# Weights of a hybrid attention block: high parts by a rounding load, low parts on VectorE, and a differential score product over all 128 rows

## The chip, the cores and the metric

The kernel runs on one core of one Trainium2 chip. The metric is the time of one execution in microseconds (us) on the device; the figure of a kernel is the median of its runs. A traced execution gives a profile: a page of totals, and rows of single instructions. Line numbers L... are those of the kernel before; where the changed kernel is spoken of, they are its own (17 to 23 lower behind `weights`).

## The reference

One decoder block over 512 tokens of width 1024, in float32:

```python
xn = rmsnorm(x, norm_mix_g)
q_lat, kv_lat, k_rope, dq, dk, dv, gate_pre = split(xn @ w_in)         # 1024 -> 4256
# branch A: latent attention, 8 heads of 64 + 32 rotary, causal
q = rmsnorm(q_lat) @ mla_w_uq ;  kv = rmsnorm(kv_lat) @ mla_w_ukv
o_mla = causal_attention([q_nope, rope(q_pe)], [k_nope, rope(k_rope)], v_mla)
# branch B: differential attention, 4 heads, two maps of 64 each, V of 128
o_diff = rmsnorm(causal_attention(q1, k1, dv) - lam * causal_attention(q2, k2, dv)) * (1 - lambda_init)
gates = sigmoid(gate_pre + b_gate)
x = x + (g_mla * (o_mla @ w_branch_mla) + g_diff * (o_diff @ w_branch_diff)) @ w_out
hn = rmsnorm(x, norm_ffn_g)
x = x + (silu(hn @ w_ffn_gate) * (hn @ w_ffn_up)) @ w_ffn_down         # hidden 2816
return rmsnorm(x, norm_final_g)
```

## The kernel before

**Two-part numbers.** TensorE multiplies in a rounded 32-bit format (float32r). To keep float32 accuracy every operand is held as a pair: a high part, which is the value rounded to that format, and a low part, which is the value minus the high part. `mm3` (L298 to L302) makes three products of each pair of operands: high by high (L300), high by low (L301), low by high (L302). Activations are split by `split` (high on ScalarE at L250 or L252, low on VectorE at L254 or L256).

**Weights.** All weights but the latent projections of the start come through `weights(src, n0, n1, pick)` (L270 to L296), a tile of up to 128 x 1024 values (512 KB) at a time. SyncE (SP) loads it as it is into a float32 tile `raw`, of which there are four. `round_hi` (L261 to L265) then writes the high part into a tile `w` (`w[:, 0]`), of which there are three, on ScalarE (L263) or VectorE (L265), and `round_lo` (L268) writes the low part (`w[:, 1]`) on GpSimd or VectorE. Which engines do it is the list `w_eng`: ScalarE and GpSimd at the start, VectorE and GpSimd from the attention on, ScalarE and VectorE in the FFN. With `pick`, only some columns of the loaded tile are rounded. A block of products of one such tile is 24 times 128 x 512 (8 row blocks of the contraction, three products each). The output projection `w_out` makes its high and low parts by lines of its own (L844 to L862). The three `w` tiles hold the latent weights first (`lat_raw`), so that the first weight tiles wait for these.

**Stages.** x is loaded, normalised through its mean square only, transposed and split; the latent projections, then MLA heads in four pairs (`mla_head`), with the projections of later heads as filling work between their steps (the lists FILL and FILL_MLA: `mqk` and `pe` are the query/key parts, `mv` and `v` the values, `qk` a differential head's query and key, `gate` a gate block); then the four differential heads (`diff_head`), filled from FILL_DIFF; then branches, `w_out`, the FFN (22 pairs of gate and up blocks, the first three of which are run on the first half of the tokens ahead of the rest, `ffn_product`), the down projection in two halves of the output (`down`), and the last norm (`finish`).

**Differential heads.** `diff_qk` (L582 to L596) projects the query and key of both maps of a head (64 rows each), rotates them (`rotate`, L561 to L567, two steps of it on GpSimd), and builds per map `m`: `q[:, m]`, in which the high part of the query lies in the map's own 64 rows and, by a DMA, once more in the other 64; `k[:, m]` with the high part of the key in its own rows and the low part in the others. So one product over 128 rows gives high·high + high·low. The low part of the query lies in `ql[own]` alone, and a second product over 64 rows gives low·high. `scores` (L627 to L645, the product at L636) runs both for each of four row blocks of 128, 256, 384 and 512 keys, for both maps; VectorE masks and takes the maximum (L640), ScalarE the exponential (L155), VectorE the reciprocal (L643) and joins the two maps (L688, L689).

**What sets the order.** The kernel's text is put into one instruction stream per engine by a scheduler that simulates a timeline; `urgent()` gives attention steps precedence. Each engine and each DMA queue works through its stream in order. A tile's name is used again in turn (L 22 buffers, raw 4, w 3, P 6, t 5; in PSUM mm 3, sc 2, tr 2, pv 1): a writer waits until the last reader of the buffer's previous content is done.

Of the kernel before, what the change touches and what calls it, by code (L numbers as in the profile page):

```python
# [13 lines left out]
F32R = mybir.dt.float32r  # L14
# [7 lines left out]
P = 128  # L22
# [22 lines left out]
W_DVE = "b0 b1 b2 b3 b4 b5 b6 b7".split()  # L45
N_WARM = 8
P_POOL = (0, 1)
W_ENG0 = ['act', 'pool']
W_ENG = ['dve', 'pool']
# [43 lines left out]
def build(ctx, nc, tc, a, out):  # L93
# [9 lines left out]
    def T(tag, shape, dtype):  # L103
        return sb.tile(shape, dtype, name=nm(tag), tag=tag, bufs=BUFS[tag])
# [16 lines left out]
    def r32(ap):  # L121
        return ap.bitcast(F32)

    def dma(o, i):
        nc.sync.dma_start(out=o, in_=i)
# [130 lines left out]
            nc.vector.scalar_tensor_tensor(out=lo, in0=src, scalar=scale, in1=r32(hi),  # L256
                                           op0=ALU.mult, op1=ALU.subtract)

    w_eng = list(W_ENG0)

    def round_hi(o, i):  # L261
        if w_eng[0] == 'act':
            nc.scalar.activation(out=o, in_=i, func=AF.Copy)  # L263
        else:
            nc.vector.tensor_copy(out=o, in_=i)  # L265

    def round_lo(o, i, hi):
        (nc.vector if w_eng[1] == 'dve' else nc.gpsimd).tensor_sub(out=o, in0=i, in1=r32(hi))  # L268

    def weights(src, n0, n1, pick=None):  # L270


        raw = T("raw", [P, 1024], F32)
        n = n0 * n1
        rv = raw[:, :n].rearrange("p (a b) -> p a b", a=n0)
        if isinstance(src, list):
            for i, s_ in enumerate(src):
                dma(rv[:, i, :].rearrange("p (h d) -> p h d", h=s_.shape[1]), s_)
        else:
            dma(rv, src)  # L280
        w = T("w", [P, 2, 1024], F32R)
        if pick is None:
            round_hi(w[:, 0, :n], raw[:, :n])
            round_lo(w[:, 1, :n], raw[:, :n], w[:, 0, :n])
        else:
            nk = sum(h * (d1 - d0) for h, d0, d1 in pick)
            wv = [w[:, s, :n0 * nk].rearrange("p (a b) -> p a b", a=n0) for s in range(2)]
            c = 0
            for h, d0, d1 in pick:
                src_ = rv.rearrange("p a (h e) -> p a h e", h=h)[:, :, :, d0:d1]  # L290
                hi, lo = [v[:, :, c:c + h * (d1 - d0)].rearrange("p a (h e) -> p a h e", h=h) for v in wv]
                c += h * (d1 - d0)
                round_hi(hi, src_)
                round_lo(lo, src_, hi)
            n = n0 * nk
# [286 lines left out]
    def diff_qk(h):  # L582


        u = diff_project(C_DQ + h * P)
        q, k = L_(), L_()
        if h % 2 == 0:
            q_lo.append(L_())
        ql = q_lo[-1][:, h % 2, :]
        for m, own, other in ((0, low, high), (1, high, low)):  # L590
            split(u[own], q[own, m, :], ql[own], DIFF_SCALE)
            dma(r32(q[other, m, :]), r32(q[own, m, :]))
        u = diff_project(C_DK + h * P)
# [4 lines left out]
    q_lo = []  # L598


    dv = []
# [207 lines left out]
    for p in range(4):  # L809
        o = L_()  # L810
        o_mla.append(o)
        w_eng[:] = W_ENG
        fill(FILL_MLA[p])
        with urgent():
            for h in range(2):
                mla_head(mqk[p], mv[p // 2], p, o, h)
# [62 lines left out]
                norm_transpose(x1[t], g_ffn, hn, t, T("L", [P, D], F32))  # L879


    w_eng[:] = ["act", "dve"]
# [119 lines left out]
```

## Time and profile before

| | |
|---|---|
| median of 3 runs | 767.74 us (767.48 to 768.22) |
| the profiled execution, its own time | 767.65 us |
| its span, from first to last instruction | 765.3 us |
| TensorE clock granted | 0.998 |
| instructions | 9589 |
| bytes read from HBM | 69.81 MB |

A row of the page's first part gives an engine's busy time, its share of the span and its instructions; PE is TensorE, PEld its weight loads, DVE VectorE, ACT ScalarE, POOL GpSimd, SP SyncE. The rows of groups give line, engine, operation, tiles written and read with their shapes, how many, then busy time and the mean of one in ns, then idle time ahead of them with what ended it. The table of windows gives the same busy times for stretches of the span, and a timeline row the start and duration of single instructions; matmuls overlap in it by their pipeline, so that the distance from start to start is what one costs.

### The profile page before, as it was taken

How to read it: one execution, taken by the hardware profiler on the slowest of the kernel's cores; microseconds unless marked ns; L12 is line 12 of the kernel's file. 1: busy time of each engine (PE TensorE's matmuls, PEld its weight loads, DVE VectorE, ACT ScalarE, POOL GpSimd, SP SyncE). 2: the span in 40 equal slices, each digit the busy share in tenths (PEclk: the TensorE clock that was granted, in tenths of full speed). 3: DMA queues.
4: the chain of work that ended last, by engine and by line, in shares of the span. 5: the costliest groups of instructions: out<-in, count | busy, mean ns of one | idle time of the engine just before them, and what ended most of it. 6: DMA issues, size and time to landing. Idle time of an engine off the chain costs nothing.

```text
span 765.3 us, 9589 instructions
## 1 busy us (share of the span) xinstructions
PE 747.1 (98%) x3639; PEld 620.6 (81%) x3639; DVE 429.9 (56%) x800; ACT 293.7 (38%) x567; POOL 167.0 (22%) x120
## 2 busy tenths in 40 slices
PE   8999999999999999999999999999999999999996
PEld 6888899887676788888889888888888888888884
DVE  6969698888999874568363333233323332223424
ACT  7464667553443421724243323232222323122314
POOL 3405343664563454430000000000000000000302
PEclk9999999999999999999999999999999999999999
DMA  9405342523222322327422332323232323232302
GB/s 309 108 1 142 98 120 72 136 69 80 72 70 57 82 83 82 110 85 253 103 83 72 94 110 83 110 83 111 83 110 83 110 85 108 87 105 87 107 0 110
DMA packets 99179, 75.67 MB, mean 99 GB/s; under 512 B 6175, under 2 KB 86845, under 8 KB 99133
## 3 DMA queue, kind: packets, MB, share of 16 engines
q1 hardware_dynamic: 99133, 75.07, 33.3%
q8 instruction: 28, 0.46, 0.3%
q14 instruction: 18, 0.15, 0.1%
HBM read 69.81 MB, written 2.10 MB: 94 GB/s over the span
## 4 chain that ended last, share of the span: by engine, by line
PE 81%; DVE 12%; issue 3%; DMA 1%; ACT 1%; POOL 1%; SPq 1%; DVEq 0%; POOLq 0%; ACTq 0%
PE ps_mm L301 22%; PE ps_mm L300 22%; PE ps_mm L302 22%; PE ps_sc L636 2%; DVE L L256 1%; PE ps_sc L301 1%; PE ps_tr L301 1%; PE ps_sc L302 1%; PE ps_tr L300 1%; PE ps_tr L302 1%; PE ps_sc L300 1%; DVE L L254 1%; PE ps_tr L662 1%; DVE w L265 1%; DVE P L688 1%
## 5 line engine op out<-in xcount | busy, mean ns | idle before, releaser
L301 PE MATMUL ps_mm<-X,w 128*128 128x512 f32 (+1 forms) x568 | 217.9, 384 | 0.0
L300 PE MATMUL ps_mm<-X,w 128*128 128x512 f32 (+1 forms) x568 | 217.7, 384 | 0.0
L302 PE MATMUL ps_mm<-X,w 128*128 128x512 f32 (+1 forms) x568 | 217.3, 383 | 0.0
L268 DVE TENSOR_TENSOR w<-raw,w 128x1024 fp32r<-128x1024 f32 x66 | 82.3, 1248 | 161.1 <-ACT w L263 161.0
L263 ACT ACTIVATE w<-raw 128x1024 fp32r<-128x1024 f32 (+1 forms) x72 | 74.0, 1031 | 160.0 <-issue 78.9
L268 POOL TENSOR_TENSOR w<-raw,w 128x1024 fp32r<-128x1024 f32 (+3 forms) x48 | 102.5, 2139 | 118.5 <-DVE w L265 36.1
L301 PEld LDWEIGHTS ps_mm<-X,w 128*128 128x128 f32 x568 | 106.9, 188 | 21.1 <-issue 0.7
L300 PEld LDWEIGHTS ps_mm<-X,w 128*128 128x128 f32 x568 | 106.7, 188 | 21.2 <-issue 1.2
L302 PEld LDWEIGHTS ps_mm<-X,w 128*128 128x128 f32 x568 | 106.9, 188 | 20.5 <-issue 0.4
L937 POOL TENSOR_TENSOR L<-L,P 128x512 f32<-128x512 f32 (+1 forms) x9 | 11.5, 1297 | 410.2 <-ACT t L936 410.1
L155 ACT ACTIVATE P<-P,sm 128x128 f32<-128x128 f32 (+3 forms) x64 | 35.9, 562 | 60.3 <-DVE sm L640 60.1
L911 DVE TENSOR_TENSOR t<-t,ps_mm 128x512 f32<-128x512 f32 x22 | 15.1, 688 | 59.7 <-PE ps_mm L302 59.7
L636 PE MATMUL ps_sc<-L,L 96*128 96x128 f32 (+11 forms) x160 | 42.6, 347 | 3.8 <-DVE sm L640 3.8
L910 ACT ACTIVATE t<-ps_mm 128x512 f32<-128x512 f32 x22 | 13.2, 599 | 80.8 <-PE ps_mm L302 80.8
L636 PEld LDWEIGHTS ps_sc<-L,L 96*128 96x128 f32 (+2 forms) x160 | 26.7, 188 | 14.8 <-issue 6.2
L301 PE MATMUL ps_mm<-w,L 128*128 128x512 f32 (+1 forms) x100 | 37.2, 372 | 0.0
L300 PE MATMUL ps_mm<-w,L 128*128 128x512 f32 (+1 forms) x100 | 37.2, 374 | 0.0
L302 PE MATMUL ps_mm<-w,L 128*128 128x512 f32 (+1 forms) x100 | 37.1, 373 | 0.0
L265 DVE CAST w<-raw 128x1024 fp32r<-128x1024 f32 (+3 forms) x42 | 36.0, 856 | 1.8 <-PE ps_mm L302 1.4
L250 ACT ACTIVATE L<-t 64x512 fp32r<-64x512 f32 (+2 forms) x47 | 29.2, 625 | 17.0 <-POOL t L566 7.3
L301 PE MATMUL ps_mm<-L,w 128*128 128x512 f32 x90 | 35.5, 394 | 0.0
L254 DVE TENSOR_TENSOR L<-t,L 128x512 fp32r<-128x512 f32 (+2 forms) x37 | 33.2, 897 | 4.0 <-ACT L L250 3.6
(264 smaller groups left out, 1269.2 us busy)
## 6 DMA issues: line engine op xcount, KB each, us to landing
raw<-w_in SPq DMA_DIRECT2D x28, 512.0 KB, 3.9
raw<-w_ffn_gate SPq DMA_DIRECT2D x22, 512.0 KB, 3.9
raw<-w_ffn_up SPq DMA_DIRECT2D x22, 512.0 KB, 3.9
raw<-w_ffn_down SPq DMA_DIRECT2D x22, 512.0 KB, 3.6
raw<-w_out SPq DMA_DIRECT2D x8, 512.0 KB, 3.6
L<-L SPq DMA_DIRECT2D x24, 128.0 KB, 2.3
L<-x SPq DMA_DIRECT2D x8, 256.0 KB, 5.7
raw<-w_branch_mla SPq DMA_DIRECT2D x4, 512.0 KB, 3.4
```

The costliest lines, as they stand in the source:

```text
L155: return nc.scalar.activation(**kw)
L250: nc.scalar.activation(out=hi, in_=src, func=AF.Copy, scale=scale)
L254: nc.vector.tensor_sub(out=lo, in0=src, in1=r32(hi))
L263: nc.scalar.activation(out=o, in_=i, func=AF.Copy)
L265: nc.vector.tensor_copy(out=o, in_=i)
L268: (nc.vector if w_eng[1] == 'dve' else nc.gpsimd).tensor_sub(out=o, in0=i, in1=r32(hi))
L300: nc.tensor.matmul(out=o, lhsT=lh, rhs=rh, start=start, stop=False)
L301: nc.tensor.matmul(out=o, lhsT=lh, rhs=rl, start=False, stop=False)
L302: return nc.tensor.matmul(out=o, lhsT=ll, rhs=rh, start=False, stop=stop)
L636: nc.tensor.matmul(out=ps[:, :n], lhsT=q[:, i * P:n], rhs=k[:, 0:n], start=j == 0, stop=j == last)
L910: last_silu = nc.scalar.activation(out=g, in_=gate_ps, func=AF.Silu)
L911: nc.vector.tensor_mul(out=g, in0=g, in1=ps)
```

## The change

`weights` loads every tile twice: the high part comes by a DMA on GpSimd's queue that writes float32 into the float32r tile `w[:, 0]` and rounds on the way; the float32 values come by SyncE into `raw` as before; VectorE makes every low part (L278). `round_hi`, `round_lo`, `w_eng`, W_ENG0 and W_ENG are gone. With `pick` only the needed columns are loaded, one DMA per row block of the contraction and queue. The rest of the loads keep their engines. `diff_qk` builds the low part of the query like the high part: in the map's own 64 rows and, by a DMA, in the other 64, in a tile of its own per head (before, two heads shared one); the second product runs over 128 rows, against the same `k[:, m]`, and so adds low·low as well.

```diff
-    w_eng = list(W_ENG0)
-
-    def round_hi(o, i):
-        if w_eng[0] == 'act':
-            nc.scalar.activation(out=o, in_=i, func=AF.Copy)
-        else:
-            nc.vector.tensor_copy(out=o, in_=i)
-
-    def round_lo(o, i, hi):
-        (nc.vector if w_eng[1] == 'dve' else nc.gpsimd).tensor_sub(out=o, in0=i, in1=r32(hi))
-
     def weights(src, n0, n1, pick=None):
...
         raw = T("raw", [P, 1024], F32)
+        w = T("w", [P, 2, 1024], F32R)
+        if pick is not None:
+            (heads, d0, d1), = pick
+            n1 = heads * (d1 - d0)
         n = n0 * n1
...
-            dma(rv, src)
-        w = T("w", [P, 2, 1024], F32R)
-        if pick is None:
-            round_hi(w[:, 0, :n], raw[:, :n])
-            round_lo(w[:, 1, :n], raw[:, :n], w[:, 0, :n])
...
+        for t, eng in ((w[:, 0, :n], nc.gpsimd), (raw[:, :n], nc.sync)):
+            v = t.rearrange("p (a b) -> p a b", a=n0)
+            if pick is not None:
+                for i in range(n0):
+                    eng.dma_start(out=v[:, i, :].rearrange("p (h d) -> p h d", h=heads),
+                                  in_=src[:, i, :].rearrange("p (h e) -> p h e", h=heads)[:, :, d0:d1])
+            elif isinstance(src, list):
+                for i, s_ in enumerate(src):
+                    eng.dma_start(out=v[:, i, :].rearrange("p (h d) -> p h d", h=s_.shape[1]), in_=s_)
+            else:
+                eng.dma_start(out=v, in_=src)
+        nc.vector.tensor_sub(out=w[:, 1, :n], in0=raw[:, :n], in1=r32(w[:, 0, :n]))
...
         u = diff_project(C_DQ + h * P)
-        q, k = L_(), L_()
-        if h % 2 == 0:
-            q_lo.append(L_())
-        ql = q_lo[-1][:, h % 2, :]
+        qs, k = [L_(), L_()], L_()
         for m, own, other in ((0, low, high), (1, high, low)):
-            split(u[own], q[own, m, :], ql[own], DIFF_SCALE)
-            dma(r32(q[other, m, :]), r32(q[own, m, :]))
+            split(u[own], qs[0][own, m, :], qs[1][own, m, :], DIFF_SCALE)
+            for q in qs:
+                dma(r32(q[other, m, :]), r32(q[own, m, :]))
...
-        return [[(q[:, m, :], k[:, m, :]), (ql[own], k[own, m, :])] for m, own in ((0, low), (1, high))]
+        return [[(q[:, m, :], k[:, m, :]) for q in qs] for m in range(2)]
```

GpSimd's stream at the end of the start, before: `w_772` is the rotary query tile (`pe`, group 0), `w_800` the second gate block, `w_831` the first values of MLA, the two 128x384 and 128x256 rows the query and key tiles of head pairs.

```order
L268 TENSOR_TENSOR w_740<-raw_738,w_740 128x256
L268 TENSOR_TENSOR w_772<-raw_768,w_772 128x384
L268 TENSOR_TENSOR w_800<-raw_798,w_800 128x1024
L268 TENSOR_TENSOR w_831<-raw_829,w_831 128x512
L268 TENSOR_TENSOR w_873<-raw_871,w_873 128x384
L268 TENSOR_TENSOR w_892<-raw_890,w_892 128x256
L268 TENSOR_TENSOR w_912<-raw_910,w_912 128x1024
```

The same place in the changed kernel, where `w_775` is the rotary query tile, `w_807` the second gate block, `w_838` the first values of MLA and `w_927` the first of the two tiles of differential values (`v`, number 0):

```order
L271 DMA w_743<-mla_w_ukv 128x2x64 x2
L275 DMA w_775<-mla_w_uq 128x4x32 x3
L277 DMA w_807<-w_in 128x8x128
L271 DMA w_838<-mla_w_ukv 128x4x64 x2
L271 DMA w_882<-mla_w_uq 128x2x64 x3
L271 DMA w_905<-mla_w_ukv 128x2x64 x2
L277 DMA w_927<-w_in 128x4x256
```

Where GpSimd subtracted, it now starts the loads of the high parts, tile by tile in the same succession; each of them waits for its buffer of `w`.

TensorE's stream where the rotary query tile is first used, before (`w_721` and `w_740` are the query and key tiles of the first head pair, `w_772` the rotary one):

```order
L302 MATMUL ps_mm_724<-L_640,w_721 128x512
L300 MATMUL ps_mm_743<-L_700,w_740 128x512
L300 MATMUL ps_mm_775<-L_624,w_772 128x512
L301 MATMUL ps_mm_775<-L_624,w_772 128x512
L302 MATMUL ps_mm_775<-L_624,w_772 128x512
L300 MATMUL ps_mm_775<-L_632,w_772 128x512
L301 MATMUL ps_mm_775<-L_632,w_772 128x512
```

And in the changed kernel (`w_720`, `w_743`, `w_775`):

```order
L285 MATMUL ps_mm_728<-L_640,w_720 128x512
L283 MATMUL ps_mm_749<-L_700,w_743 128x512
L283 MATMUL ps_mm_783<-L_624,w_775 128x512
L284 MATMUL ps_mm_783<-L_624,w_775 128x512
L284 MATMUL ps_mm_749<-L_700,w_743 128x512
L285 MATMUL ps_mm_749<-L_700,w_743 128x512
```

The rotary tile's first products stand at the same place, behind the query products of the first head pair and one key product; what moved is that the rest of the key products now stands among its own.

TensorE's stream in the changed kernel at the FFN's fourth product (`w_4093` is the tile of the third, `w_4201` that of the fourth; the third is the last that runs in two halves of 256 tokens):

```order
L285 MATMUL ps_mm_4097<-X_3707,w_4093 128x256
L283 MATMUL ps_mm_4097<-X_3707,w_4093 128x256
L284 MATMUL ps_mm_4097<-X_3707,w_4093 128x256
L285 MATMUL ps_mm_4097<-X_3707,w_4093 128x256
L283 MATMUL ps_mm_4205<-X_3706,w_4201 128x512
L284 MATMUL ps_mm_4205<-X_3706,w_4201 128x512
```

The succession is that of before; the buffer that `w_4201` takes is that of the first of the three tiles, whose last product stands 35 rows of 256 columns ahead of the first one here.

More of the change, by code (lines that the diff above doesn't have):

```diff
@@ L47 @@
 P_POOL = (0, 1)
-W_ENG0 = ['act', 'pool']
-W_ENG = ['dve', 'pool']
 FILL = [[("gate", 0, 0)], [], [("pe", 0), ("mr", 0), ("gate", 0, 1), ("mv", 0)]]
@@ L274, in weights @@
+        if pick is not None:
+            (heads, d0, d1), = pick
+            n1 = heads * (d1 - d0)
         n = n0 * n1
[L275 to L279, printed above, removed]
-            dma(rv, src)
-        w = T("w", [P, 2, 1024], F32R)
-        if pick is None:
-            round_hi(w[:, 0, :n], raw[:, :n])
-            round_lo(w[:, 1, :n], raw[:, :n], w[:, 0, :n])
[L285 to L295, printed above, removed]
+        for t, eng in ((w[:, 0, :n], nc.gpsimd), (raw[:, :n], nc.sync)):
[9 more added lines that the diff above has]
+                eng.dma_start(out=v, in_=src)
@@ L595, in diff_qk @@
             split(u[own], k[own, m, :], k[other, m, :])
-        return [[(q[:, m, :], k[:, m, :]), (ql[own], k[own, m, :])] for m, own in ((0, low), (1, high))]
-    q_lo = []
+        return [[(q[:, m, :], k[:, m, :]) for q in qs] for m in range(2)]
     dv = []
@@ L811, in build @@
         o_mla.append(o)
-        w_eng[:] = W_ENG
         fill(FILL_MLA[p])
@@ L879, in build @@
                 norm_transpose(x1[t], g_ffn, hn, t, T("L", [P, D], F32))
-    w_eng[:] = ["act", "dve"]
     def ffn_product(ps, w, c0, c1):
```

## Prediction

> **What bounds the kernel now.** I read the page's totals first, then a table of stages, then what each engine does in the stage where TensorE has company. From the page: the busy totals, the clock, the DMA queues and the chain that ended last.
>
> ```profile
> PE 747.1 (98%) x3639; PEld 620.6 (81%) x3639; DVE 429.9 (56%) x800; ACT 293.7 (38%) x567; POOL 167.0 (22%) x120
> ...
> PEclk9999999999999999999999999999999999999999
> ...
> q1 hardware_dynamic: 99133, 75.07, 33.3%
> ...
> PE 81%; DVE 12%; issue 3%; DMA 1%; ACT 1%; POOL 1%; SPq 1%; DVEq 0%; POOLq 0%; ACTq 0%
> ```
>
> TensorE is busy 747.1 of 765.3 us at an undiminished clock, so time is won by shortening its products or by filling its last 18 us, and lost wherever it is made to wait. The windows by stage (window, its length, then busy us of PE, PEld, DVE, ACT, POOL, clock, DMA share, GB/s) say where it isn't alone: start, MLA, differential attention, gates and branches, FFN.
>
> ```profile
> 0.00:50.00 50.00, 44.60 (x257) 37.69 (x258) 38.29 (x119) 32.55 (x88) 16.42 (x26) 1.00 0.51 160
> ...
> 75.00:150.00 75.00, 73.22 (x488) 67.01 (x487) 61.36 (x152) 48.76 (x116) 31.75 (x29) 1.00 0.43 111
> 150.00:280.00 130.00, 126.36 (x566) 96.08 (x565) 117.50 (x238) 53.93 (x128) 68.55 (x37) 1.00 0.28 72
> 280.00:420.00 140.00, 139.97 (x708) 119.27 (x708) 77.98 (x120) 51.31 (x87) 28.99 (x13) 1.00 0.35 110
> 420.00:640.00 220.00, 220.00 (x973) 182.15 (x972) 75.50 (x81) 64.57 (x81) 0.00 (x0) 1.00 0.33 98
> ```
>
> From 150 to 280 us VectorE has 117.5 of 130 us and TensorE idles 3.6; from 75 to 150 TensorE idles 1.8. In the FFN it idles not at all. In that crowded stage the groups of GpSimd and VectorE are:
>
> ```profile
> L268 POOL TENSOR_TENSOR w<-raw,w 128x1024 fp32r<-128x1024 f32 x16 | 40.4, 2524 | 37.8 <-DVE sm L643 15.8 <-DVE w L265 9.8 <-issue 7.2
> L265 DVE CAST w<-raw 128x1024 fp32r<-128x1024 f32 x16 | 13.7, 858 | 0.3 <-PE ps_mm L302 0.3
> L688 DVE TENSOR_SCALAR P<-P,sm,neg_lam 128x384 f32<-128x384 f32 x4 | 8.1, 2016 | 0.1
> L688 DVE TENSOR_SCALAR P<-P,sm,neg_lam 128x512 f32<-128x512 f32 x4 | 2.9, 736 | 0.0
> L256 DVE SCALAR_TENSOR_TENSOR L<-t,L 64x512 fp32r<-64x512 f32 x6 | 10.3, 1708 | 0.2 <-ACT L L250 0.2
> L256 DVE SCALAR_TENSOR_TENSOR L<-t,cols,L 128x512 fp32r<-128x512 f32 x2 | 1.5, 748 | 0.0
> ```
>
> The same L688 takes 2.02 us on 384 columns and 0.74 on 512, and L256 1.71 us on 64 partitions against 0.75 on 128: VectorE operations are stretched where GpSimd's 2.5-us subtractions lie beside them.
>
> **Second score product, 128 rows instead of 64.** The timeline of TensorE (start, us, operation) shows a 128-row product and its 64-row companion as one row "x2", on 512, 384, 256 and 128 columns, each with what follows:
>
> ```profile
> 266.71 0.82 PE L636 MATMUL ps_sc<-L,L 128*128 128x512 f32 x2
> 267.46 0.50 PE L300 MATMUL ps_mm<-X,w 128*128 128x512 f32 x1
> 267.79 0.39 PE L301 MATMUL ps_mm<-X,w 128*128 128x512 f32 x1
> 268.02 0.39 PE L302 MATMUL ps_mm<-X,w 128*128 128x512 f32 x1
> ...
> 260.42 0.70 PE L636 MATMUL ps_sc<-L,L 128*128 128x384 f32 x2
> 261.06 0.50 PE L301 MATMUL ps_mm<-X,w 128*128 128x512 f32 x1
> ...
> 226.78 0.59 PE L636 MATMUL ps_sc<-L,L 128*128 128x256 f32 x2
> 227.30 0.50 PE L301 MATMUL ps_mm<-X,w 128*128 128x512 f32 x1
> ...
> 253.60 0.47 PE L636 MATMUL ps_sc<-L,L 128*128 128x128 f32 x2
> 254.00 0.50 PE L707 MATMUL ps_tr<-L,ones_r 128*128 128x512 f32 x1
> ```
>
> From start to start an ordinary 512-column product takes 268.02 − 267.79 = 0.23, two of them 0.46; the pair takes 267.46 − 266.71 = 0.75, so 0.29 too much. For 384, 256 and 128 columns the pair takes 0.64, 0.52 and 0.40; by columns two ordinary ones would take 0.35, 0.23 and 0.12; that is 0.29, 0.29, 0.29 and 0.28 too much, and I take 0.18 for the last, since so short a product may not shrink in full proportion. Four heads with two maps make eight pairs of each size: 8 × 1.05 = 8.4 us. The product behind a pair comes 0.10 late too (267.46 to 267.79 is 0.33 for 0.23), at most 32 × 0.10 = 3.2 more; which of the two kinds of product costs it the trace doesn't say, so I take half. Sum −10.0 (bounds −8.4 and −11.6). The additional q copies (eight more of 128 KB on SP) have many microseconds until their scores; I cost them at nothing, 1 us if a head came tight.
>
> The Trainium skill, page "TensorE: Matmul & The Clock Gate", section "Packing small matmuls — row/col tiling", states that products in different row groups overlap, starting about 4 ns apart. That speaks against this edit. One place in the trace has both 64-row products side by side:
>
> ```profile
> 172.58 0.70 PE L636 MATMUL ps_sc<-L,L 128*128 128x256 f32 x3
> 173.21 0.50 PE L301 MATMUL ps_mm<-X,w 128*128 128x512 f32 x1
> ```
>
> Three products in 0.63 us, where a pair alone took 0.52: there the second half-height one was nearly free. If it held everywhere, three products would do the work of four in 16 blocks, and the edit would cost 16 × about 0.16 (the mean of 0.11 to 0.23) = 2.5 us; the four pairs above contradict it, since the order parts the two halves, and I give that 0.02.
>
> **Low parts from GpSimd to VectorE.** GpSimd loses 40.4 us between 150 and 280; VectorE loses 13.7 us of casts and gains 16 subtractions. Their duration, and the high parts that ScalarE made, from the page's groups:
>
> ```profile
> L268 DVE TENSOR_TENSOR w<-raw,w 128x1024 fp32r<-128x1024 f32 x66 | 82.3, 1248 | 161.1 <-ACT w L263 161.0
> L263 ACT ACTIVATE w<-raw 128x1024 fp32r<-128x1024 f32 (+1 forms) x72 | 74.0, 1031 | 160.0 <-issue 78.9
> ```
>
> 16 × 1.25 = 20.0. Stretching that goes is at least 4 × 1.28 (L688) + 6 × 0.96 (L256) = 10.9. So VectorE goes from 117.5 to at most 113, in a stage that TensorE wants to run through in 120: it keeps pace, barely. Of the 5.4 us that TensorE idles from 75 to 280 I take back 2 (bounds 0 and 5.4), since the chain runs through VectorE there. ScalarE loses 74 us that lay beside products: nothing.
>
> **High parts by a rounding load.** Before, the float32 tile lay in SBUF ahead of time in one of four raw buffers; once a w buffer (three) came free only 1.03 us (L263) or 0.86 (L265) and the subtraction stood ahead of the products. Now the load itself waits for the w buffer. A block needs L + 1.25 − 0.23 between that release and its first product (L from trigger to landing; one high·high product runs ahead of the low part), about 0.75 less for the small MLA tiles. Nothing of before loads on GpSimd's queue or converts on the way; the nearest rows (KB each, us to landing) are
>
> ```profile
> raw<-w_ffn_gate SPq DMA_DIRECT2D x22, 512.0 KB, 3.9
> ...
> L<-x SPq DMA_DIRECT2D x4, 512.0 KB, 8.0
> ...
> raw<-mla_w_uq SPq DMA_DIRECT2D x6, 64.0 KB, 3.8
> ```
>
> 3.9 is the same tile without conversion and alone, 8.0 a tile of that size in the crowded start, which also includes waiting behind others. I take L = 5.0, nearer the first, since the queues have room (33.3%), and keep 3.9 and 8.0. The Trainium skill, page "DMA: Bandwidth & Descriptors", fits loads issued by GpSimd with 2.0 us + bytes / 436e3, an estimate of 3.2 us here; by that only pe0 below would wait, 0.4 us, and the sum would come to about 756.
>
> Most leads are long: an FFN block is 24 products, 24 × 0.23 = 5.5 us, and the buffer of the block before last is released two blocks ahead, 10.9; the differential tiles have 11 to 15. With L = 5.0 a wide tile needs 6.0, and these don't wait. The short leads, counted from the changed order's products by these durations:
>
> - pe0's tile takes the buffer of the first gate block. In the trace of before:
>
> ```profile
> 54.54 0.39 PE L302 MATMUL ps_mm<-X,w 128*128 128x512 f32 x1
> ...
> 58.19 0.62 PE L300 MATMUL ps_mm<-L,w 128*128 128x512 f32 x2
> ```
>
>   release at 54.77 (54.54 + 0.23), first use 58.2: 3.4 us, 3.1 in the new order; need 5.3: +2.2.
> - v0's first tile: lead 4.5, need 6.0: +1.5.
> - MLA tiles: two wide ones with 5.5 and 5.7: +0.8.
> - FFN's fourth product: its buffer comes free 35 half-width products ahead, 35 × 0.12 = 4.2; need 6.0: +1.8. Two rows of that spacing, in the FFN's first blocks:
>
> ```profile
> 408.83 0.28 PE L300 MATMUL ps_mm<-X,w 128*128 128x256 f32 x1
> 408.95 0.28 PE L301 MATMUL ps_mm<-X,w 128*128 128x256 f32 x1
> ```
>
> - Three blocks where the down projection changes halves: lead 5.5, need 5.35 (four high products ahead): nothing, with no margin.
> - The first gate block's load starts beside x and the latents:
>
> ```profile
> 0.00:19.00 19.00, 15.77 (x84) 11.43 (x84) 13.03 (x43) 14.16 (x38) 7.18 (x17) 1.00 0.91 309
> ```
>
>   with the DMA engines at 91%: +0.7 (0 to 1.7).
>
> VectorE gets a new wait: each low part stands in its queue for the landing, and softmax steps, rotations and evictions queue behind it, for which score products wait. Sixteen times a fraction of a microsecond against 7 us of slack: +1.0 (0 to 6). GpSimd's queue, where the load stands where L268 stood, waits for the same release and is freed sooner than by 2.5 us of work: nothing.
>
> Sum: −10.0 − 2.0 + 2.2 + 1.5 + 0.8 + 1.8 + 0.7 + 1.0 = −4.0. The profiled execution took 767.65 (span 765.3 and 2.35 around it), 0.09 under the median of 767.74: **763.7**.
>
> **Rivals.** Each microsecond of L adds one at five places, and beyond 5.5 also at the other MLA tiles and the three blocks of the down projection.
>
> - *Faster still, about 758.* L = 3.9: the waits shrink to about 2.5, all else as above. For it: the queues are two thirds empty. Chance 0.15.
> - *The load comes late (slower).* L = 6.5: pe0 3.7, v0 3.0, k1 1.3, the other MLA tiles 4, fourth product 3.3, the down blocks 3 × 1.2, start 0.7, VectorE 2, about 21 against −12: **777**. L = 8 adds 1.5 at about twelve tiles: 795. It decides from L of about 5.5. For it: the 8.0 row, a conversion on the way, a second stream of the same size beside it; against it: 3.9. The Trainium skill, page "SBUF — State Buffer", names it the "DVE blocks DMA" trap: a DMA issued from GpSimd cannot get its descriptors written while VectorE holds their shared port in a 2-port mode. What it would do here lies within L; no run of before has such loads. Chance 0.34, with the overlap case above 0.36.
> - *No change.* VectorE at 113 of 120, waiting for landings, sets the pace of the differential stage, so that 4 to 5 of the 10 us there stay idle: 767 to 769. Chance 0.14.
> - *Throughput.* The weights are read twice now, so 33.3% becomes about 67% if both kinds of packet cost the same. If rounding packets took three times a plain one's time, 33% + 99% would be over capacity and the FFN would stretch by a third, beyond 880. Chance 0.05.
>
> The forecast has 0.30.
>
> **How the numbers follow.** A measurement here can tell 0.2% (1.5 us). Faster 0.30 + 0.15 = 0.45; same 0.14; slower 0.36 + 0.05 = 0.41. The range leaves out what is below 757, the far end of the late load above 785 and the throughput case, together about 0.2: 757 to 785. As both signs hold much, the likeliest case alone goes from 760 (L 4.4) to 766 (L 5.3).
>
> **What would show it.** Right: differential score pairs 0.46 apart on 512 columns; L688 at 0.7 us everywhere; TensorE idle before pe0, v0 and FFN's fourth product, and nowhere else in the FFN; rounding loads near 5 us. Wrong: landings above 5.5 us, idle time before many tiles put down to low parts (L278), or VectorE waiting on landings from 150 to 280.

## The result, and the profile after

The changed kernel takes 775.1 us (median of 5 runs, 772.5 to 777.51), the kernel before in the same comparison 768.22 (767.48 to 769.64): a ratio of 1.0089, 95% interval 1.0069 to 1.0109. It is slower by 6.9 us, where 763.7 was forecast; the time is inside the stated range, and the sign is that of the rival "the load comes late" (777).

The profiled execution took 775.42 us, with a span of 773.6. From its page, the lines that answer to those of before: busy totals, the clock, the two DMA queues.

```profile
PE 741.9 (96%) x3639; PEld 622.2 (80%) x3639; DVE 417.9 (54%) x806; ACT 224.3 (29%) x495; POOL 169.9 (22%) x204
...
PEclk9999999999999999999999999999999999999998
...
q0 software_dynamic: 93760, 55.71, 39.1%
q1 hardware_dynamic: 104093, 74.68, 35.2%
```

TensorE is busy 5.2 us less (747.1 before) but stands idle 31.7 of 773.6 us, where it stood 18.2. The stages, in the same windows as before (the differential stage and what follows lie some microseconds later now):

```profile
0.00:50.00 50.00, 43.42 (x248) 36.76 (x249) 39.97 (x118) 28.34 (x79) 16.89 (x29) 1.00 0.62 165
50.00:75.00 25.00, 23.19 (x124) 18.76 (x124) 19.62 (x40) 9.14 (x20) 8.20 (x11) 1.00 0.71 111
75.00:150.00 75.00, 68.66 (x451) 62.13 (x450) 53.73 (x138) 45.51 (x107) 21.90 (x34) 0.98 0.92 157
150.00:280.00 130.00, 125.64 (x614) 104.22 (x613) 108.09 (x255) 58.16 (x138) 46.19 (x42) 0.99 0.78 155
...
420.00:640.00 220.00, 220.00 (x972) 182.14 (x971) 75.43 (x80) 25.26 (x40) 34.64 (x40) 1.00 0.91 195
```

In the FFN nothing waits, as forecast, although the DMA engines are shown 91% busy. In the MLA stage (75 to 150) TensorE idles 6.3 us instead of 1.8. VectorE's busy time between 150 and 280 fell from 117.5 to 108.1, but its queue now stands at low parts for loads. What VectorE waited for from 160 to 300 us (us in total, times, longest):

```profile
DVE w L278 <- DMA w<-w_in: 19.3, 10, 4.7
```

The same of TensorE in the whole span:

```profile
PE ps_mm L283 <- DMA w<-w_in: 3.6, 3, 2.2
PE ps_sc L615 <- DMA L<-L: 3.2, 2, 2.0
PE ps_sc L615 <- DVE sm L619: 2.2, 2, 2.0
...
PE ps_mm L283 <- DMA w<-w_ffn_up: 1.3, 1, 1.3
PE ps_mm L285 <- DVE w L278: 1.3, 2, 0.8
...
PE ps_sc L283 <- DMA w<-w_ffn_down: 1.1, 1, 1.1
```

The first, fourth and sixth are waits for the new loads themselves, the fifth for low parts that stand behind such a load; with two smaller rows of that kind (0.5 and 0.2) they sum to 8.0 us. The second is for copies between rows of SBUF that stay on SyncE's queue, the third for softmax on VectorE. The landings (KB each, median us from issue):

```profile
raw<-w_in SPq DMA_DIRECT2D x28, 512.0 KB, 4.3
w<-w_in POOLq DMA_DIRECT2D x28, 512.0 KB, 5.8
...
w<-w_ffn_down POOLq DMA_DIRECT2D x22, 512.0 KB, 4.1
L<-L SPq DMA_DIRECT2D x32, 128.0 KB, 4.4
...
w<-mla_w_uq POOLq DMA_DIRECT2D x18, 64.0 KB, 2.4
```

Wide rounding loads of w_in take 5.8 us where 5.0 was assumed; the small ones are faster than assumed, 2.4, though their two or three issues stand one behind the other. The copies between SBUF rows went from 2.3 to 4.4.

All kernels issue 3639 products in nearly the same succession, so the start of the n-th product shows where time goes. Worked out from the traces, in us from the span's start; "joint" is the kernel of the experiments below with plain loads, all low parts on VectorE and 128 rows (e3_low_on_vector):

```
n        before  changed  joint   what is near it
50         14.0     14.4   14.4   start
300        57.6     59.5   57.2   first MLA projections
400        75.9     83.2   76.4   first MLA head
850       144.2    155.5  144.2   last MLA head
1400      271.2    272.2  257.0   last differential head
2100      411.8    413.7  401.2   ahead of FFN's fourth product
2200      431.6    435.8  421.1   behind it
3300      681.0    685.1  670.4   ahead of the down projection's change of halves
3500      726.3    732.4  715.7   behind it
last      757.6    763.7  747.0
```

Against before, the changed kernel loses 11.3 us up to the last MLA head, wins 10.3 back in the differential stage, and loses 0.9 in the stages behind it, 2.3 at the FFN's fourth product, 2.0 at the change of halves and 2.2 behind the last product (9.9 us to the end, 7.7 before). In that end the last two additions stand in VectorE's order behind the third token block's last steps: they start at 765.76, 1.7 us after the last product, where they started with it before.

### The profile page after: what moved, and what is told of

Same layout as the page of the kernel before. It is cut to its first block, busy times and chain, and to the rows that moved or that the text cites. A ratio compares the mean times of both kernels' runs of the same rounds, so it can differ in the third digit from the quotient of the medians.

```text
span 773.6 us, 9788 instructions
## 1 busy us (share of the span) xinstructions
PE 741.9 (96%) x3639; PEld 622.2 (80%) x3639; DVE 417.9 (54%) x806; ACT 224.3 (29%) x495; POOL 169.9 (22%) x204
## 4 chain that ended last, share of the span: by engine, by line
PE 42%; issue 9%; DMA 3%; DVE 2%; ACT 0%; DVEq 0%; POOLq 0%; ACTq 0%
PE ps_mm L285 11%; PE ps_mm L283 11%; PE ps_mm L284 11%; DMA w<-w_ffn_down 1%; PE ps_sc L284 1%; PE ps_sc L285 1%; PE ps_sc L283 1%; PE ps_tr L284 1%; PE ps_tr L283 1%; PE ps_tr L285 1%; DVE w L278 1%; DMA w<-w_ffn_up 1%; DMA w<-w_ffn_gate 1%; PE ps_pv L284 0%; PE ps_pv L283 0%
## 5 line engine op out<-in xcount | busy, mean ns | idle before, releaser
L278 DVE TENSOR_TENSOR w<-raw,w 128x1024 fp32r<-128x1024 f32 (+2 forms) x114 | 131.7, 1155 | 251.8 <-DMA w<-w_ffn_up 76.0
L277 POOL DMA_DIRECT2D w<-w_ffn_gate x22 | 19.3, 876 | 139.9 <-PE ps_mm L285 139.8
L277 POOL DMA_DIRECT2D w<-w_ffn_up x22 | 19.2, 873 | 111.4 <-PE ps_mm L285 111.4
L615 PE MATMUL ps_sc<-L,L 96*128 96x128 f32 (+7 forms) x160 | 37.7, 335 | 5.5 <-DMA L<-L 3.2
L277 POOL DMA_DIRECT2D w<-w_in x28 | 25.2, 901 | 69.2 <-PE ps_mm L285 45.9
L252 DVE TENSOR_TENSOR L<-t,L 128x512 fp32r<-128x512 f32 (+2 forms) x37 | 28.9, 783 | 14.7 <-ACT L L248 14.3
L277 POOL DMA_DIRECT2D w<-w_ffn_down x22 | 15.7, 711 | 94.0 <-PE ps_sc L285 36.3
L284 PE MATMUL ps_mm<-L,w 128*128 128x512 f32 x90 | 35.3, 394 | 0.0
L285 PE MATMUL ps_mm<-L,w 128*128 128x512 f32 x90 | 35.2, 393 | 0.0
L283 PE MATMUL ps_mm<-L,w 128*128 128x512 f32 x90 | 35.1, 391 | 0.0
```

Source lines behind the costliest of these rows:

```text
L252: nc.vector.tensor_sub(out=lo, in0=src, in1=r32(hi))
L277: eng.dma_start(out=v, in_=src)
L278: nc.vector.tensor_sub(out=w[:, 1, :n], in0=raw[:, :n], in1=r32(w[:, 0, :n]))
L283: nc.tensor.matmul(out=o, lhsT=lh, rhs=rh, start=start, stop=False)
L284: nc.tensor.matmul(out=o, lhsT=lh, rhs=rl, start=False, stop=False)
L285: return nc.tensor.matmul(out=o, lhsT=ll, rhs=rh, start=False, stop=stop)
```

## The experiments

The first theory after the result (A) was that the score product gives its 10 us and that the loads cost more than was worked out. Its rival (B) was that the time won came from GpSimd's subtractions going. A third (C) was that two streams of loads slow each other.

**Which part gains.** The kernel before with the new `diff_qk` alone (e1_rows128):

```diff
-        return [[(q[:, m, :], k[:, m, :]), (ql[own], k[own, m, :])] for m, own in ((0, low), (1, high))]
+        return [[(q[:, m, :], k[:, m, :]) for q in qs] for m in range(2)]
```

> The kernel before with the second score product over 128 rows alone; loads, high and low parts as before. Theory A (the score product gives what was worked out, the loads cost more than worked out): 757 to 760, differential score pairs on 512 columns 0.46 us apart, nothing else moved. Theory B (the time won between 155 and 272 us came from GpSimd's subtractions going, not from the score product): 765 to 768.

Measured: 765.43 us, ratio 0.9972 (0.9961 to 0.9983), 2.2 us better than before's 767.64 in that comparison. Theory A falls in the form it was put. The changed kernel with `diff_qk` of before (e2_loads_rows64):

> The changed kernel with the second score product back on 64 rows; rounding loads and low parts on VectorE stay. Theory A: 775 plus 8 to 11, so 783 to 786. Theory B: 774 to 777.

Measured: 778.85, ratio 1.0143 (1.0125 to 1.0162); against the changed kernel's 775.1 the 128 rows are worth 3.8. Next, e1 with every low part on VectorE (e3_low_on_vector):

```diff
-W_ENG0 = ['act', 'pool']
-W_ENG = ['dve', 'pool']
+W_ENG0 = ['act', 'dve']
+W_ENG = ['dve', 'dve']
```

> Rows 128 as in the first run, plain loads and high parts as before, but every low part on VectorE as in the changed kernel. Theory A: VectorE's relief from GpSimd is worth 0 to 3 us beyond the first run, 755 to 760. Theory B: it carries the gain, 5 to 10 us below the first run. If VectorE becomes the bound: 2 to 8 above the first run.

Measured: 756.14, ratio 0.9843 (0.983 to 0.9857), 9.3 below e1. And the same line in the kernel before, with 64 rows (e8_low_on_vector_rows64):

> The kernel before with every low part on VectorE and nothing else. Theory B with VectorE as the pace of the differential stage: with GpSimd out of the way TensorE is the limit there, so the score product over 64 rows costs its 8 to 10 us, 764 to 766 against 756.1 with 128 rows. If the score product is worth the 2 to 4 us of the two other comparisons everywhere: 758 to 760.

Measured: 763.47, ratio 0.9946 (0.9931 to 0.996). So the rows alone give 2.2, the low parts alone 4.7 (768.13 in that comparison), both together 11.5. With GpSimd out of the way the score product is worth 7.3, otherwise 2.2. The stage shows why: from 150 to 280 us in e1,

```profile
150.00:280.00 130.00, 120.44 (x575) 97.83 (x575) 117.96 (x239) 54.70 (x130) 68.61 (x37) 0.99 0.33 82
```

TensorE's work shrank (126.36 before), VectorE's didn't, and TensorE waits for it. Its waits from 150 to 300 us in e1:

```profile
PE ps_sc L632 <- DVE sm L636: 7.1, 6, 1.5
PE ps_tr L658 <- DVE P L685: 2.0, 1, 2.0
```

And in e3, where those are all of them:

```profile
PE ps_tr L703 <- DVE L L695: 2.5, 1, 2.5
PE ps_mm L300 <- DVE t L564: 1.2, 1, 1.2
```

The six waits for softmax are gone in e3, although VectorE does 22.2 us of subtractions more. The groups of VectorE from 150 to 280 us show what paid for it, first in e1:

```profile
L256 DVE SCALAR_TENSOR_TENSOR L<-t,L 64x512 fp32r<-64x512 f32 x6 | 10.3, 1710 | 0.2 <-ACT L L250 0.2
L684 DVE TENSOR_SCALAR P<-P,sm,neg_lam 128x384 f32<-128x384 f32 x4 | 8.1, 2022 | 0.1
```

Then the same lines and the subtractions in e3:

```profile
L268 DVE TENSOR_TENSOR w<-raw,w 128x1024 fp32r<-128x1024 f32 x17 | 22.2, 1303 | 0.1
L256 DVE SCALAR_TENSOR_TENSOR L<-t,L 64x512 fp32r<-64x512 f32 x6 | 5.9, 986 | 0.1
L684 DVE TENSOR_SCALAR P<-P,sm,neg_lam 128x384 f32<-128x384 f32 x4 | 1.9, 478 | 0.1
```

L684 falls from 2.02 to 0.48 us, L256 from 1.71 to 0.99. Summed over all operations in 150 to 280, what VectorE needs beyond the shortest of each kind is about 31 us in e1 and about 10 in e3. That agrees with the Trainium skill, page "SBUF — State Buffer", section "Who interferes with whom", by which a VectorE operation with two SBUF inputs, or in a two-port mode, and a GpSimd operation that reads SBUF exclude each other.

**Where the loads lose.** The rest, 775.1 − 756.14 = 19.0 us, is what the rounding loads cost. Three kernels use them in one part of the program only, plain loads elsewhere:

```diff
+    cast = [True]
+    def weights(*args):
+        return (weights_cast if cast[0] else weights_raw)(*args)
...
+    cast[0] = False
     o_diff, parts = [], []
```

That is e10_cast_to_mla, on the basis of e3:

> 128 rows, low parts on VectorE, rounding loads for the tiles up to the last MLA head alone (the first two differential heads' tiles among them), plain loads behind. From the traces' common places (the same count of products) the changed kernel has lost 11 of its 19 us by 144 us: 766 to 769 against 756.1 if that loss arises there. If it is made up for later, because VectorE has slack: 758 to 763.

Measured: 766.58, ratio 0.9983 (0.997 to 0.9996): 10.4 above e3. The differential heads, gates and branches alone, with `cast` true from that last line to the FFN (e11_cast_diff_branches):

> The same, rounding loads for the tiles of the last differential heads, gates and branches alone. If VectorE's waits for landings (19.3 us in ten waits between 160 and 300 us of the changed kernel) set the pace there: 759 to 763, with idle TensorE put down to VectorE between 160 and 280. If leads of 11 to 15 us hide them, as was forecast: 755 to 757.

Measured: 760.78, ratio 0.9905 (0.9892 to 0.9917): 4.6 above e3. From 150 to 300 us its TensorE waits for rotations on VectorE, which itself stands 17.8 us for loads of w_in between 160 and 300:

```profile
PE ps_mm L329 <- DVE t L593: 5.7, 3, 3.0
```

From the FFN on, with `cast` true from there, on the basis of e1 (e4_cast_from_ffn):

> Rows 128, the weights of before up to the branches, rounding loads from the FFN on. Theory A: first run plus 2.1 (FFN's fourth product) plus 2 (change of halves in the down projection) plus at most 2.2 (end), 761 to 765. If the second stream of loads cost throughput by itself: more, with idle time spread over the FFN's blocks.

Measured: 770.87, ratio 1.004 (1.0028 to 1.0053): 5.4 above e1's 765.43. The three add up to 20.4, close to the 19.0; of e4's 5.4, 1.0 stands at its start already, where its traced run waits longer for x (2.42 us for 1.68 in e1).

The products' starts and the spans say the same of the changed kernel itself. Against e3 it loses 11.3 us up to the 850th product and a net 1.2 from there to the 2100th: 3.9 are lost by the 1400th, and 2.7 come back behind it, where e3 has a wait of its own (2.5 us, for the rounded squares of the last differential head). It loses 2.2 more at the FFN's fourth product, 2.0 at the change of halves and 2.7 behind the last product: 19.4 in all (773.6 − 754.2).

**What they lose by.** e6_four_high divides the w tile and gives the high part a fourth buffer for one raw tile:

```diff
-BUFS = dict(X=2, L=22, P=6, PT=1, raw=4, w=3, t=5, sm=24)
+BUFS = dict(X=2, L=22, P=6, PT=1, raw=3, wh=4, wl=3, t=5, sm=24)
...
-        w = T("w", [P, 2, 1024], F32R)
+        wh, wl = T("wh", [P, 1024], F32R), T("wl", [P, 1024], F32R)
```

> The changed kernel with the w tile divided in a high tile (four of them) and a low tile (three), and three raw tiles instead of four, so that each rounding load may start one block earlier in the same memory. Theory A (the loads lose by waiting for a buffer): the waits ahead of the rotary tile, the differential values, the first differential query, FFN's fourth product and the down projection's change of halves go or shrink, 775 becomes 760 to 766. Theory C (two streams of loads slow everything): 772 or more, waits on plain copies stay.

Measured: 767.75 (763.45 to 771.22), ratio 0.9996 (0.9978 to 1.0013): 7.3 us of the 19 come back. In its trace no wait stands at the FFN's fourth product or at the change of halves, and from 160 to 300 us VectorE waits for no rounding load (19.3 us in the changed kernel); from the 850th to the 1400th product it loses nothing against e3, where the changed kernel loses 3.9. So from the differential stage on the loads lose by waiting for their buffer. Most of the time that comes back is behind that stage: 2.3 at the fourth product, 2.0 at the change of halves and 2.7 behind the last product. Of the 3.9, 3.2 are lost again by the 2100th product, most of it in a wait of 2.33 at the output projection, where VectorE stands for a late load of x. Up to the 850th product e6 loses 11.6, as much as the changed kernel. That doesn't clear the buffers there, since the low part still has three: at 62.06 us VectorE has stood 2.17 us for one, and TensorE then waits 2.29 us for the rotation behind it, in the place where the changed kernel waits for a load.

e7_small_as_before loads the small MLA tiles as before:

```diff
+        small = pick is not None or isinstance(src, list)
+        return (weights_raw if small else weights_cast)(src, n0, n1, pick)
```

> The changed kernel with the small MLA tiles (picked columns, rotary tile) loaded whole and rounded as before, low parts on VectorE; wide tiles keep their rounding loads. If the three or two serial issues of GpSimd per small tile and their short runs carry the loss between 58 and 145 us: 766 to 770. If the wide tiles carry it: 773 to 776.

Measured: 773.4, ratio 1.0071 (1.0053 to 1.0088): 1.7 below the changed kernel, with intervals that overlap. At the 300th product it has lost 0.9 us against e3, the changed kernel 2.3; by the 850th 10.0. The small tiles are at most a small part of it.

e12_copies_on_act_queue moves the copies between SBUF rows to ScalarE's DMA queue:

```diff
+    def copy_rows(o, i):
+        nc.scalar.dma_start(out=o, in_=i)
...
-                dma(r32(q[other, m, :]), r32(q[own, m, :]))
+                copy_rows(r32(q[other, m, :]), r32(q[own, m, :]))
...
-            dma(r32(q[64:96, :, :]), r32(pe[r0:r0 + 32, :, :]))
-            dma(r32(k[64:96, :, :]), r32(kpe))
+            copy_rows(r32(q[64:96, :, :]), r32(pe[r0:r0 + 32, :, :]))
+            copy_rows(r32(k[64:96, :, :]), r32(kpe))
```

> The changed kernel with the copies between SBUF rows (rotary rows of MLA, both halves of the differential query) on ScalarE's DMA queue instead of SyncE's. If the copies are late because they queue behind raw loads that wait for a raw tile, whose release waits for a low part and that for a rounding load: both waits of TensorE for them (1.95 and 1.27 us) go, 769 to 772. If they are late because the DMA engines are crowded: 774 to 777, the waits stay.

Measured: 775.1 (771.9 to 778.79), ratio 1.0086 (1.0059 to 1.0113). The two waits for copies are gone from its trace, so the queue was their cause (the copies land no sooner, 4.7 us for 4.4, but start earlier); at the 900th product it is 3.9 us ahead of the changed kernel; the median time is the same. A wait of 1.50 us for w_in at 86 us (the second tile of the first differential values), one of 1.77 for softmax at 183 and one of 1.82 for VectorE at 275 stand in their place. So this expectation was right on the cause and missed the time. The median decides little here: three of the six runs took 771.9 to 773.1 us at a granted clock of 0.992 to 0.995, three 777.1 to 778.8 at 0.985 to 0.987. The traced one is among the longer, with five slow stretches as described below (near 68, 184, 276, 420 and 706 us), where the changed kernel's has two.

e9_second_stream was to measure a second stream by itself, into one spare tile that nobody reads, in turn rounding and plain:

```diff
+            spare = spare if streams[0] % 2 else r32(spare)
+            nc.gpsimd.dma_start(out=spare.rearrange("p (a b) -> p a b", a=n0), in_=src)
```

> The kernel with plain loads, 128 rows and low parts on VectorE (756.1), and beside it a second load of every wide tile on GpSimd's queue into a spare tile that nobody reads, in turn rounding and plain; L tiles 21 instead of 22. It measures the second stream by itself. Theory A: nothing waits for it, 755 to 759; landings of the plain loads on SyncE's queue 4 to 5 us instead of 3.9. Theory C: 762 or more, with TensorE waiting for plain copies. A rounding load lands later than a plain one on the same queue by 0 to 1 us.

Measured: 849.8, ratio 1.1063 (1.1035 to 1.1091). This experiment was badly made: with one spare tile each load waits for the one before, and GpSimd's other work queues behind:

```profile
PE ps_tr L663 <- POOL P L775: 21.2, 4, 14.4
PE ps_tr L663 <- ACT P L777: 9.8, 2, 5.3
PE ps_tr L708 <- POOL L L701: 8.1, 3, 4.5
```

It says nothing on the two streams, but one thing on the rounding: in the down projection rounding and plain loads alternate on GpSimd's queue, and eleven in a row landed after 5.0, 5.5, 5.4, 5.0, 4.9, 5.0, 4.9, 6.1, 5.4, 5.2 and 5.0 us. All 22 lie between 4.7 and 6.1; the two kinds average 5.2 and 5.1. Rounding costs nothing that shows. GpSimd's queue is slower than SyncE's in this run (3.6 there), but not in general: in the changed kernel w_ffn_up lands after 4.7 us on GpSimd's queue and 5.4 on SyncE's, w_ffn_down after 4.1 and 4.2.

Four more kernels went at the 10.4 us up to the last MLA head, on the basis of e10. One more w tile, with 20 L tiles instead of 22 to make room (e14_four_w), and its control with plain loads (e14_plain_l20):

```diff
-BUFS = dict(X=2, L=22, P=6, PT=1, raw=4, w=3, t=5, sm=24)
+BUFS = dict(X=2, L=20, P=6, PT=1, raw=4, w=4, t=5, sm=24)
```

> Rounding loads up to the last MLA head (766.6) with four w tiles instead of three, raw still four, L 20 instead of 22 to make room. If the loads lose by waiting for a w tile: 757 to 761, if the plain kernel with 20 L tiles stays near 756. If by crowding or VectorE's queue: 764 to 767.

> The plain kernel with low parts on VectorE and 128 rows (756.1) with 20 L tiles: the control of the run before. 755 to 758 if the two tiles aren't missed.

Measured: 771.78, ratio 1.0062 (1.0045 to 1.0079), and 766.62, ratio 0.9986 (0.9976 to 0.9996). The control itself loses 10.5 us, in one wait of 4.1 us ahead of the FFN and in the down projection, so the two tiles are missed. The difference of the two is 5.2, but by the traces the fourth tile wins little where it should: at the 850th product e14_four_w has lost 8.3 us against e3, e10 9.0. Its wait for the second gate block's load is gone, and 2.28 us for VectorE's rotation stand in the same place, VectorE having stood 1.30 for that load. Inconclusive.

Without the plain loads beside the rounding ones (e15_no_raw_stream), and with a low part that doesn't read the high part (e16_low_without_wait):

```diff
-        for t, eng in ((w[:, 0, :n], nc.gpsimd), (raw[:, :n], nc.sync)):
+        for t, eng in ((w[:, 0, :n], nc.gpsimd),):
...
-        nc.vector.tensor_sub(out=w[:, 1, :n], in0=raw[:, :n], in1=r32(w[:, 0, :n]))
+        nc.vector.tensor_sub(out=w[:, 1, :n], in0=r32(w[:, 0, :n]), in1=r32(w[:, 0, :n]))
```

```diff
-        nc.vector.tensor_sub(out=w[:, 1, :n], in0=raw[:, :n], in1=r32(w[:, 0, :n]))
+        nc.vector.tensor_sub(out=w[:, 1, :n], in0=raw[:, :n], in1=raw[:, :n])
```

> Rounding loads up to the last MLA head (766.6), without the plain loads beside them: the low part subtracts the high part from itself, so low parts of these weights are zero. Half of the bytes go, the waits for a w tile stay. If two streams crowd each other: 757 to 761, rounding loads landing below 4.5 us. If the waits for a w tile cost: 764 to 767.

> Rounding loads up to the last MLA head (766.6); the low part subtracts the raw tile from itself (low parts of these weights are zero) and so VectorE no longer waits for the rounding load, while TensorE still does. If VectorE's queue standing still at the low parts costs the time: 758 to 761. If TensorE's own waits for the high part do: 764 to 767.

Measured: 763.8, ratio 0.9952 (0.994 to 0.9964), and 767.83, ratio 0.9995 (0.998 to 1.0009). Leaving out half of the bytes gives 2.8 of the 10.4: the wait for the first differential query's tile shrinks from 2.47 to 0.80, the copies are no longer waited for, and wide rounding loads land after 4.8 instead of 5.5. Taking VectorE's wait for the load away gives nothing there (767.83, e10 766.58).

**A version that beats both.** In e3 the longest wait left is 2.5 us for VectorE's rounded squares in the last differential head (L695). e13_squares_on_scalar lets ScalarE make them:

```diff
-        nc.vector.tensor_copy(out=sqs[0], in_=sq)
+        nc.scalar.activation(out=sqs[0], in_=ps, func=AF.Square)
```

> The fastest so far (128 rows, plain loads, low parts on VectorE, 756.1) with the rounded squares of a differential head's output made by ScalarE instead of VectorE: the 2.45-us wait of TensorE for them (last differential head) and the slow stretch behind it go: 752 to 754. If VectorE's order shifts against it: 756 to 758.

Measured: 753.53 (752.79 to 754.86), ratio 0.9813 (0.98 to 0.9825), the fastest: 128 rows and low parts on VectorE, without rounding loads. The wait for the squares is gone; one of 1.72 us for an eviction on VectorE stands near its place.

## Why the prediction was wrong, point by point

- **The gains, −12.0 in sum: right in sum, wrong in their parts.** Together they are worth 11.5 (e3). The split into −10.0 for the score product and −2.0 for GpSimd's relief was wrong: singly they are worth 2.2 and 4.7, and neither sum is the joint one. TensorE's price was right within its bounds: from start to start the 64 score products take 18.9 us before and 10.4 in e3, and the product behind a pair takes mostly 0.33 and 0.23, which comes to about 11, nearer the bound of −11.6 than the −10.0 taken. What was missed is that VectorE sets the stage's pace in the kernel before. "It keeps pace, barely" was said of the changed kernel and holds; that the score product alone would be worth next to nothing without the relief wasn't seen. Of the stretching only the two groups shown were counted, 10.9; it was about 21.
- **The Trainium skill's packing rule** ("TensorE: Matmul & The Clock Gate", section "Packing small matmuls — row/col tiling") did not decide here: with the order that this program gets, 64-row products cost 7.3 us (e8 against e3), since their two halves don't stand side by side.
- **The loads, +8.0: this is the term that failed; it was 19.0.** Item by item against e3: the tiles and the start up to the last MLA head were put at 5.2 (2.2 + 1.5 + 0.8 + 0.7) and cost 11.3; VectorE's wait 1.0 and a net 1.2; the FFN's fourth product 1.8 and 2.2; the change of halves 0 and 2.0; the end behind the last product stood in no step and cost 2.7. Of its steps:
  - *L = 5.0.* The rows show 5.8 for w_in, up to 7.7 in the crowded MLA stage. The fit of the Trainium skill ("DMA: Bandwidth & Descriptors", section "Anatomy of one DMA — SWDGE (gpsimd) path"), an estimate of 3.2, is further off: 4.1 to 5.8 by tensor. (The sum of 756 put beside that fit leaves out the +0.7 and +1.0 of the sum for the start and VectorE.)
  - *Leads.* The FFN's fourth product (+1.8; 1.29 and 0.47) came as worked out in sum, from a lead and a landing that were both shorter (3.5 us for 4.2, 4.7 for 5.0). The rotary tile wasn't waited for at all (+2.2): it comes in three small loads, each landing in 2.4 to 2.8 us. Nor was the first gate block's (+0.7). v0 (+1.5) wasn't waited for either: its load landed after 6.3 us, at 81.53, and TensorE came to it at 81.66, because it had stood 1.95 us for copies just before; in e12, without that wait, its two tiles cost 0.23 and 1.50. The second gate block's tile, which the steps don't name, waited 1.8 (1.00 and 0.81). The first differential query waited 2.2, where 0.8 stood for two wide tiles of that stage together, because its load landed after 7.7. The change of halves, "nothing, with no margin", cost 2.
  - *VectorE's new wait, +1.0 (0 to 6).* It stands 19.3 us in ten waits between 160 and 300. The step counted "a fraction of a microsecond" for each; it is 1.9. Alone this costs 4.6 us (e11); in the changed kernel 3.9 by the 1400th product (e6 takes them away), of which 2.7 come back behind it. So the net of 1.2 meets the +1.0 by luck, through a wait that e3 has there and the changed kernel hasn't. That the low part's place in VectorE's order was planned for an earlier landing is likely and not shown.
  - *SyncE's queue.* It was not among the steps. Copies between SBUF rows stand behind raw loads, these wait for a raw tile, that for a low part, and that now for a rounding load. 3.2 us of waits, shown by e12; the median time didn't fall when they went.
- **What a stall costs.** Each wait was priced at its length. After the longer ones TensorE runs slowly for a while. From the timeline behind the wait for the first differential query's tile, and the table of windows there and at a wait of 2.04 us at 221:

```profile
142.52 0.47 PE L283 MATMUL ps_mm<-X,w 128*128 128x512 f32 x1 [2.20 <-DMA w<-w_in]
142.83 0.54 PE L284 MATMUL ps_mm<-X,w 128*128 128x512 f32 x1
143.16 0.95 PE L762 MATMUL ps_pv<-PT,L 128*128 128x512 f32 x2
143.91 1.48 PE L641 MATMUL ps_tr<-ident,P 128*128 128x128 f32 x6
145.04 0.78 PE L285 MATMUL ps_mm<-X,w 128*128 128x512 f32 x1
145.62 0.63 PE L283 MATMUL ps_mm<-X,w 128*128 128x512 f32 x1
146.05 0.53 PE L284 MATMUL ps_mm<-X,w 128*128 128x512 f32 x1
146.41 0.39 PE L285 MATMUL ps_mm<-X,w 128*128 128x512 f32 x1
146.65 0.40 PE L283 MATMUL ps_mm<-X,w 128*128 128x512 f32 x1
```

```profile
140.00:150.00 10.00, 7.80 (x32) 6.39 (x31) 7.82 (x12) 3.83 (x8) 1.81 (x2) 0.83 1.60 252
...
144.00:145.00 1.00, 1.00 (x7) 1.00 (x6) 0.97 (x3) 0.21 (x1) 0.00 (x0) 0.50 2.78 302
...
220.00:230.00 10.00, 8.61 (x34) 7.28 (x35) 9.43 (x24) 4.02 (x10) 3.75 (x3) 0.83 0.52 106
```

  Products of 512 columns start 0.31 to 0.58 us apart instead of 0.23 until 146.4, and the granted clock of those 10 us is 0.83; by single microseconds it is 0.50 from 143 to 146 and 1.00 again from 147. From 142.52 to 146.41 are 3.9 us; the five products, two of L762 and six transposes that start in it take 7 × 0.23 and 6 × 0.1 = 2.2 us elsewhere. So the stall costs 1.7 us more than its 2.2, and the one at 221 about as much. The kernel before has no such stretch ahead of its last product. But e3 has two as well, behind its waits of 1.18 us at 187 and 2.45 at 263.5, so against e3 they move the loss to an earlier place and don't add to the 19.0.
- **The loss up to the last MLA head is named in its parts, not in one cause.** In the changed kernel's trace these are the later start of the tables (a wait of 1.64 us at 44.8, 0.60 before, so 1.0 more), the second gate block's tile (1.8), copies (1.95 and 1.27), a pair of short waits at 113 (0.9), the first differential query (2.2) and the slow stretch behind it (1.7): 10.8 in sum. By the products' starts 11.3 are lost, although a wait of 1.48 us for softmax that before has at 77.9 is gone, so some 2 us have no row of their own. None of the experiments that took one of them away won it back whole; the next wait took its place. What makes all of them late at once stays open, and so does the cause of the largest part of the loss; leaving half of the bytes out gives a quarter.
- **The rival "the load comes late"** had the sign and, at 777, nearly the time, but not the way: it needed L = 6.5 and waits ahead of many tiles. L was 5.8 at most by tensor, and only 8.0 of the 19.0 are direct waits for tiles and their low parts. The prediction gave this rival more chance (0.34) than its own forecast (0.30), and two of its signs of being wrong came: landings above 5.5 us, and VectorE waiting on landings between 150 and 280.

## What to carry to other kernels

A load that can start only when its final buffer is free has lost the staging buffer's lead: price it from the release, and price it again for the engine that stands in order behind it, not only for the one that uses the data. Two edits that relieve two engines of one stage are to be priced together: where both are nearly full, either alone gives little. And an engine that is off the path can still stretch the one on it: compare one operation's duration in different company before its work is called free.

## What the runs showed of the hardware that was not expected

- A rounding load is no slower than a plain one on the same queue (e9: 4.7 to 6.1 us, 5.2 and 5.1 on average, 512 KB). Which queue is slower differs: in e9 GpSimd's (5.0, SyncE's 3.6), in the changed kernel GpSimd's for w_in (5.8 and 4.3) and SyncE's for w_ffn_up (5.4 and 4.7).
- GpSimd is occupied 0.7 to 1.1 us for the issue of each load, of 64 KB as of 512 KB.
- After idle times of TensorE of 1.2 to 2.5 us a slow stretch of three to four microseconds followed (granted clock 0.50 from 143 to 146 us), worth 1.7 us. It isn't a plain threshold: a wait of 1.95 us at 78.9 us in the changed kernel has none, one of 1.18 at 187 us in e3 and one of 1.73 at 271.7 us in e8 have.
- DMA engines shown over 90% busy through the FFN (share 0.91) made TensorE wait for nothing from 420 to 640 us, though SyncE's loads of w_ffn_gate and w_ffn_up landed after 5.1 and 5.4 us instead of 3.9. The share doesn't say that bandwidth is spent: at the same 0.91, 309 GB/s were moved in the first 19 us of the kernel before, and 195 here.
